# Near scores of a pair in one step, far turns in pairs, and group weights through main memory

## The chip, the cores and the metric

One core of one Trainium2 chip. The metric is the device time of the whole kernel in microseconds, the median of the runs; beside it stands one profiled execution, with its own time and its span (first to last instruction). TensorE's clock was granted nearly in full throughout (0.99 to 1.00 in every stretch read here, the level of 2.4 GHz).

## The reference, cut to what matters

A decoder trunk of two residual layers on 512 tokens of 1024 features. Layer 0 mixes tokens by pooling, layer 1 by attention; each is followed by a SwiGLU feed-forward block. Only the attention of layer 1 matters here.

```python
ATTN_PATTERNS = ((128, 1), (512, 4), (2048, 16))       # window, dilation; heads 0-5, 6-10, 11-15
def attn_mixer(h, w_qkv, w_out):
    ...
    q = rope(qkv[:, :, 0]) * HEAD_DIM ** -0.5
    k = rope(qkv[:, :, 1])
    v = qkv[:, :, 2]
    for (window, dilation), n_g in zip(ATTN_PATTERNS, HEAD_GROUPS):
        o_g, lse_g = dilated_window_attention(q[:, :, sl], k[:, :, sl], v[:, :, sl], window, dilation)
        outs.append(o_g)
        lses.append(jax.nn.logsumexp(lse_g, axis=-1) - math.log(n_g))
    alpha = jax.nn.softmax(jnp.stack(lses, axis=-1), axis=-1)
    merged = jnp.concatenate([o_g * (N_ATTN_GROUPS * alpha[:, :, g])[:, :, None, None] for g, o_g in enumerate(outs)], axis=2)
    ...
    return jnp.einsum('bse,ed->bsd', merged, w_out)
```

So every token has a softmax within each head (window of 128 for the near heads 0 to 5; every fourth token for the far heads 6 to 10, every sixteenth for 11 to 15), and a weight for each of the three groups of heads (alpha), which multiplies that group's outputs.

## The kernel before

All large products run as three fp32r products of parts (high x high, low x high, high x low), so TensorE has about three times the plain work; a weight tile is loaded by SP (L104), its high part cast by ScalarE (L137), its low part taken by VectorE (L138). TensorE's order is the order of the program text (L76). The order on VectorE, ScalarE and POOL is the planner's, which starts from the program's order and a model of when things are ready.

Attention is laid out in **steps**, one per projection. Steps 0 to 15 project q and k of the eight head pairs t (step 2t for q, 2t+1 for k, L962 to L973): `project` (L226) is 24 matmuls of 512 columns into one of four PSUM banks of the pool `mm`. `rope` (L812) takes such a bank: VectorE shuffles and multiplies, POOL multiplies (L817), VectorE adds. Steps 16 to 18 project v for the near heads, steps 19 to 26 the far heads' v in two parts of four steps with 320 columns. After each step `later` (L929) puts some of the attention's own work on TensorE between the projections:

- **Scores.** `near_scores` (L840) runs for pairs t = 0, 1, 2 in two halves, blocks 0 and 1 at step 2t+3 and blocks 2 and 3 at step 2t+4, each half with two banks of the pool `psc` (which has two). VectorE adds the mask (L859, L865) and takes the row maxima (L862, L863, L869). `far_scores` (L873) does a far pair (t = 3 to 7) at step 2t+3 with the same two banks.
- **Softmax.** `soften` (L832): VectorE negates the maxima (L835), ScalarE takes exponentials (L837). One step later `normalise` (L896): VectorE takes reciprocals, POOL multiplies (L902 for near heads, L904 for far ones).
- **Turns.** `transposes` (L907), one step after that at the earliest: seven blocks of a near head or four of a far head are turned by TensorE through the pool `ptr` (two banks, four blocks each) and copied to `pT` by ScalarE for even heads (L925), by VectorE for odd ones (L923). `later` takes one head per step, in the order of the heads: steps 6 to 21.
- **Values.** `turn` (L1045) turns the near heads' v tiles at steps 17, 18 and 19 through `ptr` as well, ahead of `later`; ScalarE copies them (L1050).
- **Group weights.** At step 20 `group_sums` (L979), at step 22 `group_weights` (L999): VectorE computes `gw`, 12 columns for each token, and POOL copies each group's four columns out to 512 (L1019). At step 24 `spread_weights` (L1023) multiplies these by the identity on TensorE (L1028), and ScalarE copies the results to `LB`, which then holds each token's weight on all partitions (L1031).

Then (L1090 on) each pair's outputs are products of v and pT, which VectorE multiplies by `LB` (L1112 near, L1115 far); they are split (L312, L313) and go into the output projection (L352 to L354), and the feed-forward block follows.

Of the kernel before, what the change touches and what calls it, by code (L numbers as in the profile page):

```python
# [10 lines left out]
F32 = mybir.dt.float32  # L11
# [6 lines left out]
P = 128  # L18
S = 512
# [38 lines left out]
def trunk_kernel(ctx: ExitStack, tc: tile.TileContext, x_in, xT, gam, gains, consts, ident_d, w0, wT, w1, wv, w_down, out):  # L58
# [731 lines left out]
    with ExitStack() as actx:  # L790
        ap = actx.enter_context(tc.tile_pool(name="attn", bufs=1, reuse_waits="tile"))
        work = ExitStack()
        aw = work.enter_context(tc.tile_pool(name="attnw", bufs=2, reuse_waits="tile"))
        psc = actx.enter_context(tc.tile_pool(name="psc", bufs=2, space=bass.MemoryType.PSUM))
# [45 lines left out]
        def near_scores(t, half, q, k):  # L840

            pair = (2 * t, 2 * t + 1)
            if half == 0:
                state[t] = [aw.tile([P, 4, 256], F32, name="e", bufs=4) for _ in pair]
            scs = [psc.tile([P, 4, P], F32, name="sc").rearrange("p b k -> p (b k)") for _ in pair]
            for b in (2 * half, 2 * half + 1):
                at = (b % 2) * 256
                lo = max(b - 1, 0) * P
                for i, scf in enumerate(scs):
# [6 lines left out]
            for h, scf, e in zip(pair, scs, state[t]):  # L856
                flat = e.rearrange("p b k -> p (b k)")
                if half == 0:
                    nc.vector.scalar_tensor_tensor(  # L859
                        flat[:, P : 4 * P], scf[:, P : 4 * P], HD ** -0.5, masks[:, 0 : 3 * P], op0=ALU.mult, op1=ALU.add  # L860
                    )
                    nc.vector.tensor_reduce(mx[:, h, 0:1], e[:, 0, P:], axis=AX.X, op=ALU.max)  # L862
                    nc.vector.tensor_reduce(mx[:, h, 1:2], e[:, 1, :], axis=AX.X, op=ALU.max)  # L863
                else:
                    nc.vector.scalar_tensor_tensor(  # L865
                        e[:, 2:4, :], scf.rearrange("p (b k) -> p b k", b=2), HD ** -0.5,
                        masks[:, P : 3 * P].unsqueeze(1).to_broadcast([P, 2, 2 * P]), op0=ALU.mult, op1=ALU.add,
                    )
                    nc.vector.tensor_reduce(mx[:, h, 2:4], e[:, 2:4, :], axis=AX.X, op=ALU.max)  # L869
                    got.append((h, *soften(h, e, [e[:, b, (P if b == 0 else 0) : 256] for b in range(4)])))  # L870
# [58 lines left out]
        def later(step):  # L929

            if pend_tr and pend_tr[0][0] <= step:
                transposes(*pend_tr.pop(0)[1:])
# [29 lines left out]
        for t in range(8):  # L962
# [7 lines left out]
            if t < 3:  # L970
                pend_sc += [(at, near_scores, (t, 0, q, k)), (at + 1, near_scores, (t, 1, q, k))]
            else:
                pend_sc.append((at, far_scores, (t, q, k)))  # L973
# [3 lines left out]
        state["perm"] = ap.tile([P, 4, 2], F32, name="gperm")  # L977

# [20 lines left out]
        def group_weights():  # L999
# [8 lines left out]
            w = ap.tile([P, 3, 4], F32, name="gw")  # L1008
# [7 lines left out]
            bcs = []  # L1016
            for g in range(3):
                bc = aw.tile([P, S], F32, name="ropeb" if g == 2 else "ropea").rearrange("p (b j) -> p b j", b=4)
                nc.gpsimd.tensor_copy(bc, w[:, g, :].unsqueeze(2).to_broadcast([P, 4, P]))  # L1019
                bcs.append(bc)  # L1020
            return bcs

        def spread_weights(bcs):  # L1023

            for g, bc in enumerate(bcs):
                tp = psc.tile([P, 4, P], F32, name="sc") if g == 2 else ptr.tile([P, 4, P], F32, name="tp")
                for b in range(4):
                    nc.tensor.matmul(tp[:, b, :], lhsT=bc[:, b, :], rhs=ident, start=True, stop=True)  # L1028

                to = LB[g].rearrange("p (j r) -> p r j", r=R) if g == 0 else LB[g].rearrange("p (r j) -> p r j", r=R)  # L1030
                nc.scalar.copy(to, tp)  # L1031
# [159 lines left out]
```

## Time and profile before

| what | value |
|---|---|
| median of 3 runs | 1018.32 us (1017.35 to 1019.07) |
| the profiled execution | 1018.4 us, span 1016.6 us |
| TensorE busy | 1000.0 us (98%) |
| VectorE busy | 792.8 us (78%) |
| ScalarE busy | 530.0 us (52%) |
| POOL busy | 121.0 us (12%) |
| HBM read | 151.99 MB |
| the chain that ended last | 92% TensorE, 3% VectorE, 2% DMA, 2% ScalarE |

The span starts with layer 0 (to about 455 us), then come the attention (to about 680 us, its output projection among it) and the feed-forward block of layer 1. The shares are means over stages with different limits; the attention's steps, from 481 to 621 us, are where the changed lines stand. Times in a timeline are counted from the span's start. A matmul's duration in a row includes its way through the array, so the pitch from one start to the next says what it costs, not the duration.

### The profile page before, as it was taken

How to read it: one execution, taken by the hardware profiler on the slowest of the kernel's cores; microseconds unless marked ns; L12 is line 12 of the kernel's file. 1: busy time of each engine (PE TensorE's matmuls, PEld its weight loads, DVE VectorE, ACT ScalarE, POOL GpSimd, SP SyncE). 2: the span in 40 equal slices, each digit the busy share in tenths (PEclk: the TensorE clock that was granted, in tenths of full speed). 3: DMA queues.
4: the chain of work that ended last, by engine and by line, in shares of the span. 5: the costliest groups of instructions: out<-in, count | busy, mean ns of one | idle time of the engine just before them, and what ended most of it. 6: DMA issues, size and time to landing. Idle time of an engine off the chain costs nothing.

```text
span 1016.6 us, 16615 instructions
## 1 busy us (share of the span) xinstructions
PE 1000.0 (98%) x6582; PEld 912.5 (90%) x6582; DVE 792.8 (78%) x1134; ACT 530.0 (52%) x836; POOL 121.0 (12%) x108
## 2 busy tenths in 40 slices
PE   9999989999999999999999999999999999999997
PEld 7888879989998998989777899889998999999895
DVE  6483689898888788777988747569989888888875
ACT  5572467545654554463344444357654564455454
POOL 0000101101011100001333210100101001111000
PEclk9999989999999999999999999999999999999999
DMA  9451467759559854514311246525866955975522
GB/s 346 157 186 21 117 194 193 175 170 260 142 129 248 222 142 139 183 57 145 103 42 52 75 124 175 116 63 160 203 150 192 237 149 118 287 187 138 154 71 83
DMA packets 76349, 155.16 MB, mean 153 GB/s; under 512 B 6448, under 2 KB 6576, under 8 KB 76272
## 3 DMA queue, kind: packets, MB, share of 16 engines
q1 hardware_dynamic: 58944, 121.00, 35.5%
q0 software_dynamic: 17040, 32.84, 19.1%
q8 instruction: 51, 0.84, 0.3%
q10 hardware_dynamic: 288, 0.27, 0.1%
q14 instruction: 26, 0.21, 0.1%
HBM read 151.99 MB, written 2.10 MB: 152 GB/s over the span
## 4 chain that ended last, share of the span: by engine, by line
PE 92%; DVE 3%; DMA 2%; ACT 2%; issue 1%; POOL 0%; SPq 0%; ACTq 0%; POOLq 0%
PE p L601 24%; PE r L601 13%; PE r L684 10%; PE mm L601 6%; PE p L684 5%; PE mm L222 4%; PE mm L224 3%; PE mm L223 3%; PE mm L738 3%; PE mm L684 2%; PE mm L354 2%; PE mm L352 2%; PE mm L353 2%; DMA vraw<-w 1%; PE mm L1073 1%; PE mm L1072 1%
## 5 line engine op out<-in xcount | busy, mean ns | idle before, releaser
L138 DVE TENSOR_TENSOR wlo<-wraw,whi 128x1024 fp32r<-128x1024 f32 (+2 forms) x190 | 220.4, 1161 | 76.6 <-ACT whi L137 76.0
L137 ACT CAST whi<-wraw 128x1024 fp32r<-128x1024 f32 (+2 forms) x190 | 185.2, 978 | 173.0 <-issue 34.7
L137 ACT CAST whi<-vraw 128x1024 fp32r<-128x1024 f32 (+1 forms) x102 | 99.4, 976 | 148.0 <-DVE vraw L140 51.6
L601 PE MATMUL p<-t_hi,wlo 128*128 128x256 f32 x528 | 149.9, 284 | 0.0
L601 PE MATMUL p<-t_lo,whi 128*128 128x256 f32 x528 | 149.9, 284 | 0.0
L601 PE MATMUL p<-t_hi,whi 128*128 128x256 f32 x528 | 148.7, 282 | 0.9 <-ACT ct L616 0.9
L138 DVE TENSOR_TENSOR wlo<-vraw,whi 128x1024 fp32r<-128x1024 f32 (+1 forms) x102 | 114.9, 1127 | 19.8 <-ACT whi L137 19.3
L601 PE MATMUL r<-h_hi,whi 128*128 128x256 f32 x352 | 100.3, 285 | 3.9 <-ACT h_hi L312 3.9
L601 PE MATMUL r<-h_lo,whi 128*128 128x256 f32 x352 | 101.1, 287 | 0.1
L601 PEld LDWEIGHTS p<-t_hi,whi 128*128 128x128 f32 x528 | 100.1, 189 | 1.1 <-ACT ct L616 1.1
L601 PE MATMUL r<-h_hi,wlo 128*128 128x256 f32 x352 | 101.0, 287 | 0.0
L601 PEld LDWEIGHTS p<-t_hi,wlo 128*128 128x128 f32 x528 | 99.8, 189 | 0.0
L601 PEld LDWEIGHTS p<-t_lo,whi 128*128 128x128 f32 x528 | 99.3, 188 | 0.1
L106 POOL DMA_DIRECT2D wraw<-w x22 | 26.8, 1216 | 429.3 <-DMA wraw<-w 93.2
L140 DVE TENSOR_TENSOR vraw<-vraw,wraw 128x1024 f32<-128x1024 f32 x68 | 76.6, 1127 | 0.8
L601 PEld LDWEIGHTS r<-h_hi,whi 128*128 128x128 f32 x352 | 67.9, 193 | 4.1 <-ACT h_hi L312 4.1
L601 PEld LDWEIGHTS r<-h_lo,whi 128*128 128x128 f32 x352 | 67.4, 191 | 0.4 <-DVE h_lo L313 0.4
L601 PEld LDWEIGHTS r<-h_hi,wlo 128*128 128x128 f32 x352 | 67.6, 192 | 0.0
L222 PE MATMUL mm<-h_hi,whi 128*128 128x512 f32 (+1 forms) x176 | 65.3, 371 | 0.0
L224 PE MATMUL mm<-h_hi,wlo 128*128 128x512 f32 (+1 forms) x176 | 63.6, 361 | 0.0
L223 PE MATMUL mm<-h_lo,whi 128*128 128x512 f32 (+1 forms) x176 | 63.5, 361 | 0.0
L684 PE MATMUL r<-wlo,u_hi 128*128 128x512 f32 x144 | 56.1, 390 | 0.0
(313 smaller groups left out, 2516.4 us busy)
## 6 DMA issues: line engine op xcount, KB each, us to landing
wraw<-w SPq DMA_DIRECT2D x116, 512.0 KB, 4.9
wraw<-w_down SPq DMA_DIRECT2D x32, 512.0 KB, 3.7
wraw<-w POOLq DMA_DIRECT2D x22, 512.0 KB, 7.5
vraw<-w SPq DMA_DIRECT2D x22, 512.0 KB, 5.0
vraw<-w POOLq DMA_DIRECT2D x22, 512.0 KB, 8.9
wraw<-wT SPq DMA_DIRECT2D x16, 512.0 KB, 3.8
wraw<-w_down SPq DMA_DIRECT2D x24, 256.0 KB, 2.7
vraw<-w_down SPq DMA_DIRECT2D x6, 512.0 KB, 5.4
```

The costliest lines, as they stand in the source:

```text
L106: nc.gpsimd.dma_start(dst, more, accum_op=ALU.add)
L137: nc.scalar.copy(hi[:, :n], raw[:, :n])
L138: nc.vector.tensor_sub(lo[:, :n], raw[:, :n], hi[:, :n].bitcast(F32))
L140: nc.vector.tensor_add(raws[into][:, :n], raws[into][:, :n], raws[more][:, :n])
L222: nc.tensor.matmul(ps, lhsT=whi, rhs=xhi, start=first, stop=False, **kw)
L223: nc.tensor.matmul(ps, lhsT=whi, rhs=xlo, start=False, stop=False, **kw)
L224: nc.tensor.matmul(ps, lhsT=wlo, rhs=xhi, start=False, stop=last, **kw)
L352: nc.tensor.matmul(ps, lhsT=xhi, rhs=w[0][:, k, :], start=first, stop=False)
L353: nc.tensor.matmul(ps, lhsT=xhi, rhs=w[1][:, k, :], start=False, stop=False)
L601: nc.tensor.matmul(ps[:, g, :], lhsT=w[:, g, c, :], rhs=xx[:, c, :], start=i in (0, 1, 3) and g + c + k == 0, stop=c == 3 and k == 2, skip ...
L684: nc.tensor.matmul(acc[t], lhsT=u, rhs=w, start=i in (0, 1, 3) and c + k == 0, stop=c == len(pairs) - 1 and k == 2, skip_group_check=True,)
L738: nc.tensor.matmul(ps, lhsT=u, rhs=w[:, m, :], start=z + m + k == 0, stop=z == 1 and m == 1 and k == 2,)
```

## The change

Three things change in the attention, and nothing outside it.

1. A near pair is scored in one step (2t+3) with four banks: two of `psc` and two of `mm`. Masks and maxima follow per head; one reduction covers blocks 1 to 3. A near head's turn can therefore come one step earlier (steps 5 to 10).
2. `later` turns up to two heads per step where they are far heads: pairs t = 3 to 7 at steps 11, 13, 15, 17 and 19, which is two steps behind their scores.
3. The group weights are computed at step 21. At step 22 one transpose brings them to 12 rows of 128 (group and residue x token), ScalarE copies these, a DMA on POOL's queue stores them in main memory, and three more on that queue load each group's 512 values onto all 128 partitions. The values now stand by residue for all three groups, so the near heads' multiply reads and writes with a stride.

```diff
--- before.py
+++ after.py
@@ -791,6 +791,7 @@
         ap = actx.enter_context(tc.tile_pool(name="attn", bufs=1, reuse_waits="tile"))
         work = ExitStack()
         aw = work.enter_context(tc.tile_pool(name="attnw", bufs=2, reuse_waits="tile"))
+        dram = actx.enter_context(tc.tile_pool(name="dram", bufs=1, space=bass.MemoryType.DRAM))
         psc = actx.enter_context(tc.tile_pool(name="psc", bufs=2, space=bass.MemoryType.PSUM))
         ptr = actx.enter_context(tc.tile_pool(name="ptr", bufs=2, space=bass.MemoryType.PSUM))
 
@@ -837,37 +838,37 @@
                 nc.scalar.activation(blk, blk, AF.Exp, bias=neg[:, b : b + 1], accum_out=den[:, h, b : b + 1])
             return e, blocks
 
-        def near_scores(t, half, q, k):
+        def near_scores(t, q, k):
 
             pair = (2 * t, 2 * t + 1)
-            if half == 0:
-                state[t] = [aw.tile([P, 4, 256], F32, name="e", bufs=4) for _ in pair]
-            scs = [psc.tile([P, 4, P], F32, name="sc").rearrange("p b k -> p (b k)") for _ in pair]
-            for b in (2 * half, 2 * half + 1):
+            banks = [
+                [(psc.tile([P, 4, P], F32, name="sc") if half == 0 else mm.tile([P, S], F32, name="mm").rearrange("p (b k) -> p b k", b=4)) for _ in pair]
+                for half in range(2)
+            ]
+            banks = [[sc.rearrange("p b k -> p (b k)") for sc in scs] for scs in banks]
+            for b in range(4):
                 at = (b % 2) * 256
                 lo = max(b - 1, 0) * P
-                for i, scf in enumerate(scs):
+                for i, scf in enumerate(banks[b // 2]):
                     rows = slice(HD * i, HD * i + HD)
                     nc.tensor.matmul(
                         scf[:, at + (P if b == 0 else 0) : at + 256], lhsT=q[rows, b * P : (b + 1) * P],
                         rhs=k[rows, lo : (b + 1) * P], start=True, stop=True,
                     )
             got = []
-            for h, scf, e in zip(pair, scs, state[t]):
+            for i, h in enumerate(pair):
+                e = aw.tile([P, 4, 256], F32, name="e", bufs=4)
                 flat = e.rearrange("p b k -> p (b k)")
-                if half == 0:
-                    nc.vector.scalar_tensor_tensor(
-                        flat[:, P : 4 * P], scf[:, P : 4 * P], HD ** -0.5, masks[:, 0 : 3 * P], op0=ALU.mult, op1=ALU.add
-                    )
-                    nc.vector.tensor_reduce(mx[:, h, 0:1], e[:, 0, P:], axis=AX.X, op=ALU.max)
-                    nc.vector.tensor_reduce(mx[:, h, 1:2], e[:, 1, :], axis=AX.X, op=ALU.max)
-                else:
-                    nc.vector.scalar_tensor_tensor(
-                        e[:, 2:4, :], scf.rearrange("p (b k) -> p b k", b=2), HD ** -0.5,
-                        masks[:, P : 3 * P].unsqueeze(1).to_broadcast([P, 2, 2 * P]), op0=ALU.mult, op1=ALU.add,
-                    )
-                    nc.vector.tensor_reduce(mx[:, h, 2:4], e[:, 2:4, :], axis=AX.X, op=ALU.max)
-                    got.append((h, *soften(h, e, [e[:, b, (P if b == 0 else 0) : 256] for b in range(4)])))
+                nc.vector.scalar_tensor_tensor(
+                    flat[:, P : 4 * P], banks[0][i][:, P : 4 * P], HD ** -0.5, masks[:, 0 : 3 * P], op0=ALU.mult, op1=ALU.add
+                )
+                nc.vector.scalar_tensor_tensor(
+                    e[:, 2:4, :], banks[1][i].rearrange("p (b k) -> p b k", b=2), HD ** -0.5,
+                    masks[:, P : 3 * P].unsqueeze(1).to_broadcast([P, 2, 2 * P]), op0=ALU.mult, op1=ALU.add,
+                )
+                nc.vector.tensor_reduce(mx[:, h, 0:1], e[:, 0, P:], axis=AX.X, op=ALU.max)
+                nc.vector.tensor_reduce(mx[:, h, 1:4], e[:, 1:4, :], axis=AX.X, op=ALU.max)
+                got.append((h, *soften(h, e, [e[:, b, (P if b == 0 else 0) : 256] for b in range(4)])))
             return got
 
         def far_scores(t, q, k):
@@ -928,8 +929,12 @@
 
         def later(step):
 
-            if pend_tr and pend_tr[0][0] <= step:
-                transposes(*pend_tr.pop(0)[1:])
+            for _ in range(2):
+                if pend_tr and pend_tr[0][0] <= step:
+                    h, e = pend_tr.pop(0)[1:]
+                    transposes(h, e)
+                    if HEAD_GROUP[h] == 0:
+                        break
             while pend_nm and pend_nm[0][0] <= step:
                 _, h, e, blocks = pend_nm.pop(0)
                 pend_tr.append((step + 1, h, normalise(h, e, blocks)))
@@ -967,14 +972,12 @@
             k = rope(pk, t, "k")
             later(2 * t + 1)
             at = 2 * t + 3
-            if t < 3:
-                pend_sc += [(at, near_scores, (t, 0, q, k)), (at + 1, near_scores, (t, 1, q, k))]
-            else:
-                pend_sc.append((at, far_scores, (t, q, k)))
+            pend_sc.append((at, near_scores if t < 3 else far_scores, (t, q, k)))
 
         LB = [ap.tile([P, S], F32, name=f"LB{g}") for g in range(3)]
         state["sums"] = ap.tile([P, 2, 3, 4], F32, name="gsums")
         state["perm"] = ap.tile([P, 4, 2], F32, name="gperm")
+        state["w"] = ap.tile([P, 3, 4], F32, name="gw")
 
         def group_sums():
 
@@ -1005,7 +1008,7 @@
             nc.vector.tensor_max(top, top, ms[:, 0, 2, :])
             nc.vector.tensor_sub(ms[:, 0, :, :], ms[:, 0, :, :], top.unsqueeze(1).to_broadcast([P, 3, 4]))
             nc.scalar.activation(ms[:, 0, :, :], ms[:, 0, :, :], AF.Exp)
-            w = ap.tile([P, 3, 4], F32, name="gw")
+            w = state["w"]
             for g, n in enumerate(GROUP_HEADS):
                 nc.vector.scalar_tensor_tensor(w[:, g, :], ms[:, 1, g, :], 1.0 / n, ms[:, 0, g, :], op0=ALU.mult, op1=ALU.mult)
             nc.vector.tensor_add(top, w[:, 0, :], w[:, 1, :])
@@ -1013,31 +1016,26 @@
             nc.vector.reciprocal(top, top)
             for g in range(3):
                 nc.vector.scalar_tensor_tensor(w[:, g, :], w[:, g, :], float(len(GROUP_HEADS)), top, op0=ALU.mult, op1=ALU.mult)
-            bcs = []
+
+        def spread_weights():
+
+            tp = ptr.tile([P, 4, P], F32, name="tp")
+            nc.tensor.transpose(tp[:12, 0, :], state["w"].rearrange("p g r -> p (g r)"), ident)
+            rows = aw.tile([P, S], F32, name="ropea")[:, :P]
+            nc.scalar.copy(rows[:12, :], tp[:12, 0, :])
+            far = dram.tile([12, P], F32, name="far")
+            nc.gpsimd.dma_start(far, rows[:12, :])
             for g in range(3):
-                bc = aw.tile([P, S], F32, name="ropeb" if g == 2 else "ropea").rearrange("p (b j) -> p b j", b=4)
-                nc.gpsimd.tensor_copy(bc, w[:, g, :].unsqueeze(2).to_broadcast([P, 4, P]))
-                bcs.append(bc)
-            return bcs
-
-        def spread_weights(bcs):
-
-            for g, bc in enumerate(bcs):
-                tp = psc.tile([P, 4, P], F32, name="sc") if g == 2 else ptr.tile([P, 4, P], F32, name="tp")
-                for b in range(4):
-                    nc.tensor.matmul(tp[:, b, :], lhsT=bc[:, b, :], rhs=ident, start=True, stop=True)
-
-                to = LB[g].rearrange("p (j r) -> p r j", r=R) if g == 0 else LB[g].rearrange("p (r j) -> p r j", r=R)
-                nc.scalar.copy(to, tp)
+                nc.gpsimd.dma_start(LB[g], far[4 * g : 4 * g + 4, :].rearrange("(o r) j -> o (r j)", o=1).partition_broadcast(P))
 
         def between(step):
             later(step)
             if step == 20:
                 group_sums()
+            if step == 21:
+                group_weights()
             if step == 22:
-                state["bcs"] = group_weights()
-            if step == 24:
-                spread_weights(state["bcs"])
+                spread_weights()
 
 
         to_turn = []
@@ -1108,11 +1106,9 @@
                     continue
                 rows = slice(0, P) if both else slice(HD * (h % 2), HD * (h % 2) + HD)
                 al = LB[HEAD_GROUP[h]]
-                if h < 6:
-                    nc.vector.tensor_mul(o[rows, :], ps[rows, :], al[rows, :])
-                else:
-                    by_r = lambda z: z[rows, :].rearrange("p (r j) -> p r j", r=R)
-                    nc.vector.tensor_mul(o[rows, :].rearrange("p (j r) -> p r j", r=R), by_r(ps), by_r(al))
+                by_r = lambda z: z[rows, :].rearrange("p (r j) -> p r j", r=R)
+                in_turn = lambda z: z[rows, :].rearrange("p (j r) -> p r j", r=R)
+                nc.vector.tensor_mul(in_turn(o), in_turn(ps) if h < 6 else by_r(ps), by_r(al))
             split(m_hi[:, t, :], m_lo[:, t, :], o)
         norm = Norm(2, mp.tile([P, D], F32, name="even_rows"))
         sc_tile = lambda: psc.tile([P, 4, P], F32, name="sc")
```

## Rows read from the trace of the kernel before

**Rows 1.** Windows: length; busy us (and instructions) of each engine; clock, DMA share, GB/s
```profile
480.00:541.93 61.93, 60.34 (x322) 47.24 (x320) 55.19 (x104) 27.35 (x80) 21.85 (x17) 1.00 0.21 70
640.00:1016.60 376.60, 369.48 (x2518) 343.98 (x2516) 303.30 (x411) 200.50 (x278) 36.55 (x32) 0.99 0.58 152
```
**Rows 2.** Timeline of TensorE (start, us, engine, line, operation): steps 4 and 7
```profile
482.53 0.50 PE L222 MATMUL mm<-h_hi,whi 128*128 128x512 f32 x1
489.27 0.50 PE L222 MATMUL mm<-h_hi,whi 128*128 128x512 f32 x1
...
504.09 0.39 PE L222 MATMUL mm<-h_hi,whi 128*128 128x512 f32 x1
...
508.64 0.39 PE L224 MATMUL mm<-h_hi,wlo 128*128 128x512 f32 x1
```
**Rows 3.** Timeline of TensorE: the spread at step 24 and the next product
```profile
611.06 1.95 PE L1028 MATMUL tp<-ident,ropea 128*128 128x128 f32 x16
...
613.65 0.39 PE L1072 MATMUL mm<-whi,h_hi 128*128 128x320 f32 x1
```
**Rows 4.** Timeline of TensorE: its two waits, at steps 8 and 11
```profile
517.02 0.70 PE L851 MATMUL sc<-k,q 64*128 64x256 f32 x2
518.36 1.13 PE L851 MATMUL sc<-k,q 64*128 64x256 f32 x6 [0.65 <-DVE e L859]
...
539.93 0.98 PE L920 MATMUL tp<-ident,e 128*128 128x128 f32 x7 [0.94 <-ACT pT L925]
```
**Rows 5.** VectorE by line (ns min/median/max; the split's row: total, mean ns)
```profile
L859 DVE SCALAR_TENSOR_TENSOR e<-sc,gain x6: 527/546/599, 483.9 to 517.8; 128x384 f32<-128x384 f32 x6
L862 DVE TENSOR_REDUCE mx<-e x6: 253/276/285, 485.6 to 519.4; 128x1 f32<-128x128 f32 x6
L863 DVE TENSOR_REDUCE mx<-e x6: 403/406/411, 485.8 to 519.6; 128x1 f32<-128x256 f32 x6
L869 DVE TENSOR_REDUCE mx<-e x6: 667/669/678, 493.6 to 525.5; 128x2 f32<-128x512 f32 x6
L138 DVE TENSOR_TENSOR wlo<-wraw,whi 128x1024 fp32r<-128x1024 f32 (+2 forms) x190 | 220.4, 1161 | 76.6 <-ACT whi L137 76.0
```
**Rows 6.** Timelines of TensorE and ScalarE: value turns at steps 17 and 19
```profile
579.70 0.60 PE L1049 MATMUL tp<-ident,ropea 128*128 128x128 f32 x4
580.82 0.59 ACT L1050 COPY v<-tp 128x512 f32<-128x512 f32 x1
591.72 0.60 PE L1049 MATMUL tp<-ident,ropea 128*128 128x128 f32 x4
592.55 0.58 ACT L1050 COPY v<-tp 128x512 f32<-128x512 f32 x1
```
**Rows 7.** Landing of a store (L759) and a POOL load (L961); weights; multiplies
```profile
DMA to landing us min/median/max: 2.0/2.0/2.0
DMA to landing us min/median/max: 4.0/4.0/4.0
598.98 1.17 POOL L1019 COPY ropea<-gw 128x512 f32<-128x512 f32 x2 [9.82 <-DVE gw L1015]
623.79 0.69 DVE L1112 TENSOR_TENSOR o<-mm,LB 128x512 f32<-128x512 f32 x1 [0.52 <-PE mm L1103]
L1115 DVE TENSOR_TENSOR o<-mm,LB x6: 1056/1078/1122, 629.4 to 638.0; 128x512 f32<-128x512 f32 x4, 64x512 f32<-64x512 f32 x2
```
**Rows 8.** Timelines: POOL's products, and TensorE's first product behind far scores
```profile
498.17 2.97 POOL L902 TENSOR_TENSOR e<-e,rden 128x768 f32<-128x768 f32 x2 [0.96 <-DVE rden L899]
526.96 0.50 PE L222 MATMUL mm<-h_hi,whi 128*128 128x512 f32 x1
539.95 1.05 POOL L904 TENSOR_TENSOR e<-e,rden 128x512 f32<-128x512 f32 x1
555.05 0.50 PE L222 MATMUL mm<-h_hi,whi 128*128 128x512 f32 x1
565.15 1.05 POOL L904 TENSOR_TENSOR e<-e,rden 128x512 f32<-128x512 f32 x1
```

## The prediction

> **What bounds the kernel now.** I read the busy time of the engines over the attention stretch first, then TensorE's own order of work, and only then the engines that feed it. TensorE works almost without a break: in [rows 1] it is busy for 60.34 of the 61.93 us in which the near pairs are scored, and 369.48 of 376.60 us behind the attention. So a microsecond of TensorE's work or waiting taken out of the attention should reach the end nearly whole. The reader is to see a second thing in the same row: VectorE is busy 55.19 of those 61.93 us. It is the engine that could take over there, and TensorE's waits in this stretch [rows 4] are waits for what VectorE delivers late. Before the near pairs and after the last far pair nothing of the kind shows.
>
> **The change part by part.** All sums are against the profiled execution: 1018.4 us, of which 1016.6 us are the span. The median of the runs is 1018.32 us, 0.08 us lower, so a sum carries over as it is.
>
> *Spreading the group weights.* TensorE loses 24 matmul pieces, from 611.06 to 613.65 [rows 3]: 2.59 us, 0.108 us a piece. It gains one transpose, one such piece, with its own way in and out of the fp32 work (some 0.03 us in all by the same rows, as 24 pieces leave no room for more). I take 2.59 - 0.11 - 0.03 = **2.45 us** gained. The three copies on POOL and the three on ScalarE that go lie beside TensorE's work; I cost them at nothing.
>
> *The broadcast.* Instead the weights go ScalarE copy, store to main memory, three loads, the four DMAs one behind the other on POOL's queue. No row shows that pair of transfers; the nearest ones are a store that landed in 2.0 us and a 320 KB load from POOL's queue that landed in 4.0 us [rows 7] (the new loads are 256 KB each). The group weights are ready at 598.98 [rows 7], where POOL begins to copy them. Even if the transpose came no earlier than the old spread at 611.06, the copy (0.59 us, like the one in [rows 6]), the store and the first load would end at 611.06 + 0.11 + 0.59 + 2.0 + 4.0 = 617.8, and its place is two part-projects earlier. The first reader is VectorE's multiply at 623.79 [rows 7]. At least 6 us of cover, so nothing on the path. If the cover were gone, VectorE's multiplies would wait, then the PSUM banks they free, then TensorE. What is queued behind these DMAs on POOL is the accumulating weight loads of the FFN, which start later. TensorE's multiplications don't see the new strided multiply for heads 0 to 5 either: it goes from 0.69 us to at most about the 1.08 us of the far heads' form [rows 7], 3 x 0.39 = 1.2 us on VectorE, beside products that read finished tiles. One rule speaks against this part. Rows 7 show one POOL load alone, nothing about what VectorE does to it. The Trainium skill, "SBUF — State Buffer", section "SBUF: two separate sides", says that a DMA issued from POOL's queue can be kept from writing its descriptors while VectorE runs certain copies, and advises another queue. No row here shows that; by an estimate of one 0.69 us instruction ahead of each of the four DMAs it would make the rows some 2.8 us later, and leave the sum as it is.
>
> *Near scores in one step.* Each pair is scored at step 2t+3 alone instead of in halves at two steps. The products are the same. What goes is one entry and exit per pair: 24 products of a projection have a pitch of (508.64 - 504.09)/20 = 0.2275 us, 5.46 us in all [rows 2]. The step with a second half lasts from 482.53 to 489.27, 6.74 us, so the half costs 1.28 us, while its 8 pieces at 0.107 are 0.86. The difference, 0.42 us, is the separate block's own price; three pairs give **1.26 us**. Bounds: 0.2 us a pair, if the second half's long exit stays with the merged block, to 0.42.
>
> *VectorE's part of it.* One reduction over 256 columns (0.406 us) and one over 512 (0.669 us) [rows 5] become one over 768. Their difference, 0.263 us for 256 columns, makes that 0.93 us: 0.14 us less a head, 0.85 us over six heads, none of it on the path by itself.
>
> *Waits that should go.* Two stalls of TensorE stand in the rows [rows 4]. At 517.02 two pieces are issued, then none until 518.36, where the row names VectorE's first mask: 1.34 - 2 x 0.107 = 1.13 us. The cause is that a half takes both score banks again one step after the half before it. With four banks a pair comes back to the same two banks only two steps later, so this goes. At 539.93 a transpose waits 0.94 us for ScalarE's copy of the head before; that copy stands behind the exponentials of the first far pair, which VectorE let start late. Near work ends one step earlier after the change, and the last near head turns at step 10, before those exponentials. I take both: **2.07 us**. Bounds: 1.13 to 2.07.
>
> *Banks.* The two further banks come from the four that projections use. A projection then waits for the rope of two projections ago instead of four. VectorE's backlog would have to exceed 5.5 us before that costs anything, and the rows of masks and reductions [rows 5] come to some 2 to 2.5 us a head. I cost it at nothing; without that cover it would be the excess of the backlog, a microsecond at most.
>
> *Far turns in pairs.* Both heads of a far pair turn at one step, every second step. The transposes are the same; that fewer entries are made I cost at nothing (0 to 0.15 us). But at steps 17 and 19 the turn of a value tile comes first, and three tiles then want two banks. The third waits for ScalarE's copy of the first. At step 17 the turn starts at 579.70 and the copy runs 580.82 + 0.59 = 581.41 [rows 6]; the third tile would be wanted at 579.70 + 8 x 0.108 = 580.57, so **0.85 us** are lost. At step 19 the turn starts at 591.72, the copy ends at 592.55 + 0.58 = 593.13, the third tile is wanted at 592.58: **0.55 us**. In sum 1.4 us lost; between 0 (if ScalarE takes the copy first) and 2.5.
>
> *The deadline.* Turns now come exactly two projections behind the scores: about 11.0 us, plus 0.43 us for the second head, whose first head turns ahead of it. Near pairs: today the chain from the second half's scores (over at 489.27) to POOL's first finished head (498.17 + 2.97/2 = 499.66) is 10.4 us [rows 2, 8]. In it the masks stand in program order behind the next projection's rope and a weight split (1.16 us a split [rows 5]); now they stand ahead of both, and that makes up for the first half's 0.546 + 0.276 + 0.406 = 1.23 us of that head, so I expect 10 to 11 us. In the steady far stretch the scores end at 555.05 and POOL's last product at 565.15 + 1.05 = 566.20 [rows 8]: 11.15 us against 11.4, just in time. I put **0.5 us** down for misses; bounds 0 and the rival below.
>
> Sum: 2.45 + 1.26 + 2.07 - 1.4 - 0.5 = 3.9 us gained, 1018.4 - 3.9 = **1014.5 us**.
>
> **The rivals.** *The masks queue as they do now.* The near chain of 10.4 us has the first half's masks outside it. If VectorE handles all masks of the pair before the first maximum, 2 x 1.23 = 2.46 us come on top: 12.85 us against 11.0, a miss of 1.85 us. Three pairs: up to 5.5 us, though the later two have another head's seven transposes (0.75 us) in the time available. The first far pair, with scores ending at 526.96 and POOL at 539.95 + 1.05 = 541.00, takes 14.0 us today [rows 8] against about 12.2. That would be 4 to 5 us of new stalls and eat the gain: **1018.6 us**. For it: VectorE is 89% busy there, its order is a planner's, and today it lets a weight split pass between a pair's masks. Against: the masks' place in program order and the work taken away.
>
> *VectorE becomes the bound, and it is slower.* The same place, but each of six pairs' masks (three near, three far) has another weight split (1.16 us [rows 5]) ahead of it in VectorE's queue, which today falls into the slack between halves. Then the misses are 5 + 6 x 1.16 = 12 us: 1018.4 + 12 + 1.4 - 5.8 = 1026 us at full price, where 5.8 us is the sum of the gains and 1.4 us the value tiles' loss, and about **1022 us** if two thirds of it happen. It decides from the point at which the misses exceed 4.4 us (5.8 - 1.4); past 6.4 us it shows as slower. For it speaks that VectorE has only 6.7 us of slack in 61.93; against, that the same work fits today with two stalls of 2.07 us.
>
> *The change does only what the trace proves.* Stalls neither go nor come: 1018.4 - 2.45 - 1.26 = **1014.7 us**, close enough to the forecast to share its range. *No new stall at all*: 1018.4 - 5.8 = **1012.6 us**. *The broadcast is late* by over 6 us: each microsecond beyond costs one, **1020 us**.
>
> **How the numbers follow.** Forecast, with the rival that shares its range: 0.58 (1013 to 1016.2). No new stall: 0.09. Masks queue as now: 0.20, mostly within 0.2% (2 us, about what a measurement of this kernel can tell from no change). VectorE bound: 0.10. Broadcast late: 0.03. Faster: 0.58 + 0.09 = 0.67; same 0.21, most of the queueing case; slower 0.12. The range reaches from 1012.0 (no new stall, with the 0.15 us of fewer entries and up to 0.4 us in the 0.85 us that VectorE saves) to 1018.8, the whole of the queueing case; left out are the slower cases and a little below.
>
> **What would show it.** The spread's pieces gone and one transpose in their place (right by construction, 2.4 us). Three blocks of 16 score pieces of about 1.9 us, with no wait between. No idle at the fourth near scores or at the fourth head's copy. A wait of 0.5 to 0.9 us for the value tile's copy at each of steps 17 and 19. The three broadcasts landed before the first multiply. Wrong: waits of transposes for POOL at steps 5 to 15 that sum to over 3 us (the queueing case), projections that wait for rope (banks), or multiplies that wait for a DMA.

## The result, and the profile after

The changed kernel takes 1022.24 us (median of 6 runs, 1020.37 to 1023.65), the kernel before 1018.16 us beside it: a ratio of **1.0036, interval 1.0023 to 1.005**. It is slower by some 3.7 us, where 3.9 us less were forecast. The gains came as forecast (5.8 us, seen in the run g3 below); what failed is a term that stood in the sum with 0.5 us.

A stretch of TensorE's timeline places it better than the whole time does: from the first score product of step 3 to the first output product. Each kernel has one profiled execution, so a length has no interval of its own; but the stretch begins anywhere from 480.39 to 483.56 us in the fourteen profiles, though no edit touches what lies ahead of it, while waits that several kernels share come out alike (the one at step 5 below: 0.72 to 0.75 us in eight kernels). In the kernel before this is 620.86 - 481.68 = 139.18 us. In the changed kernel (timeline of TensorE: start, us, engine, line, operation):

```profile
482.74 0.49 PE L854 MATMUL sc<-k,q 64*128 64x128 f32 x4
...
625.15 0.32 PE L1099 MATMUL mm<-pT,v 128*64 128x128 f32 x1
```

That is 142.41 us, 3.23 us more. The profiled spans differ by 3.9 us: a further 1.06 us lie ahead of the stretch (482.74 against 481.68), in the first matmuls of the kernel, which the change doesn't touch (see the end), and 0.4 us less lie behind it. The lengths below are all of this stretch.

Where the 3.23 us come from is seen in what TensorE waited for, first as its weight loads' waits in the stretch (us in total, times, longest):

```profile
PEld tp L921 <- DVE pT L924: 2.8, 3, 1.0
PEld tp L921 <- POOL e L905: 2.7, 1, 2.7
PEld tp L921 <- issue: 1.8, 2, 1.0
PEld tp L921 <- DVE e L902: 1.1, 1, 1.1
```

Every large one ends at a transpose (L921): TensorE is ready to turn a head, and the head or the bank is not. Then one by one, with the releaser in brackets; these answer [rows 4] and [rows 6]:

```profile
496.38 0.98 PE L921 MATMUL tp<-ident,e 128*128 128x128 f32 x7 [0.73 <-DVE e L902]
...
511.34 0.66 PE L921 MATMUL tp<-ident,e 128*128 128x128 f32 x4 [0.34 <-DVE pT L924]
512.80 0.55 PE L921 MATMUL tp<-ident,e 128*128 128x128 f32 x3 [0.81 <-DVE pT L924]
...
528.24 0.55 PE L921 MATMUL tp<-ident,e 128*128 128x128 f32 x3 [0.80 <-DVE pT L924]
...
544.77 0.66 PE L921 MATMUL tp<-ident,e 128*128 128x128 f32 x4 [2.51 <-POOL e L905]
...
587.11 0.63 PE L921 MATMUL tp<-ident,e 128*128 128x128 f32 x4 [0.82 <-ACT v L1048]
...
599.85 0.63 PE L921 MATMUL tp<-ident,e 128*128 128x128 f32 x4 [0.52 <-ACT v L1048]
```

Steps 5, 7, 9, 11, 17 and 19. The two waits of [rows 4] are gone, and waits at six steps stand in their place. The last two are the value tiles' copies, as forecast. The windows around step 11 show a second cost (length; busy us and instructions of PE, PEld, DVE, ACT, POOL; granted clock, DMA share, GB/s):

```profile
541.66:545.36 3.70, 1.19 (x9) 0.78 (x7) 3.38 (x7) 1.53 (x2) 2.51 (x2) 1.00 0.17 16
545.36:549.00 3.64, 3.64 (x22) 3.03 (x22) 3.12 (x6) 0.00 (x0) 0.58 (x1) 0.55 0.21 78
```

A far pair's eight transposes take 3.70 us up to the scores behind them, against 0.96 us at step 13 of the same kernel (559.06 to 560.02): 2.7 us of waiting. Behind them the granted clock is at about half, the lower of its two levels (1.2 GHz), for 3.6 us: the scores take 1.72 us instead of 1.09 and the two next projections 11.98 us instead of 11.02, 1.6 us together. Step 11 costs 4.3 us in all.

The parts that were to gain did gain. The spread is one transpose (0.27 us in its row, 0.02 us to the next product's start), and the broadcast was in time: its store landed 3.5 us after issue, its loads 6.5 to 7.5 us after theirs, the last at 617.6 + 7.5 = 625.1 at the latest, before the first multiply at 629.48. These answer [rows 7] and [rows 3]:

```profile
L1023 PE MATMUL tp<-ident,gw x1: 271/271/271, 610.9 to 610.9; 128*12 128x128 f32 x1
...
DMA to landing us min/median/max: 3.5/3.5/3.5
...
L1029 POOL DMA_DIRECT2D LB<-far x3: 544/544/577, 616.5 to 617.6; - x3
...
DMA to landing us min/median/max: 6.5/7.0/7.5
...
629.48 2.06 DVE L1111 TENSOR_TENSOR o<-mm,LB 128x512 f32<-128x512 f32 x2
```

VectorE's rows answer [rows 5]: the merged reduction takes 0.938 us (0.93 forecast).

```profile
L870 DVE TENSOR_REDUCE mx<-e x6: 935/938/944, 488.5 to 522.5; 128x3 f32<-128x768 f32 x6
```

### The profile page after: what moved, and what is told of

Read it like the earlier page. It is cut to its first block, busy times and chain, and to the rows that moved or that the text cites. A ratio compares the mean times of both kernels' runs of the same rounds, so it can differ in the third digit from the quotient of the medians.

```text
span 1020.5 us, 16564 instructions
## 1 busy us (share of the span) xinstructions
PE 999.7 (98%) x6559; PEld 911.9 (89%) x6559; DVE 796.1 (78%) x1128; ACT 529.0 (52%) x834; POOL 125.1 (12%) x109
## 4 chain that ended last, share of the span: by engine, by line
PE 89%; DVE 5%; ACT 2%; DMA 2%; issue 2%; POOL 1%; SPq 0%; POOLq 0%; DVEq 0%; ACTq 0%
PE p L601 24%; PE r L601 13%; PE r L684 10%; PE mm L601 6%; PE p L684 5%; PE mm L222 3%; PE mm L738 3%; PE mm L223 3%; PE mm L224 3%; PE mm L684 2%; PE mm L352 2%; PE mm L354 2%; PE mm L353 2%; DMA vraw<-w 1%; PE early L223 1%
## 5 line engine op out<-in xcount | busy, mean ns | idle before, releaser
L684 PE MATMUL r<-whi,u_lo 128*128 128x512 f32 x144 | 56.1, 390 | 0.0
```

Of the source, the lines that this page charges most:

```text
L684: nc.tensor.matmul(acc[t], lhsT=u, rhs=w, start=i in (0, 1, 3) and c + k == 0, stop=c == len(pairs) - 1 and k == 2, skip_group_check=True,)
```

## The experiments

**The two theories.** A: the merged near step costs the time, since the masks of a whole pair stand in VectorE's queue at once and what TensorE needs stands behind them. B: the turns of far heads in pairs cost it, since two projections are too short a deadline for both heads. The planner orders VectorE, ScalarE and POOL anew for every kernel, so an edit can also move instructions that it doesn't name; at two places below (g2 and g3) that is seen to matter. The lengths, and the time against the kernel before in the same set of runs (the two agree to 1.4 us in every row):

| kernel | parts | stretch, us | time ratio (interval) |
|---|---|---|---|
| before | | 139.18 | 1 |
| changed | all three | 142.41 | 1.0036 (1.0023 to 1.005) |
| e1 | near step | 139.04 | 1.0002 (0.9988 to 1.0016) |
| e2 | far pairs | 142.28 | 1.0035 (1.0022 to 1.0049) |
| e3 | spread | 136.60 | 0.9974 (0.9961 to 0.9987) |
| e4 | near step, spread | 136.49 | 0.9987 (0.9975 to 1.0) |
| f1 | e4, near copies on ScalarE | 135.36 | 0.9964 (0.9949 to 0.9979) |
| f2 | changed, far turns a step later | 136.98 | 0.998 (0.9965 to 0.9995) |
| f3 | changed, value tiles in other banks | 139.12 | 1.0012 (0.9995 to 1.0029) |
| f4 | changed, with all three of these | 135.28 | 0.9961 (0.9946 to 0.9975) |
| g1 | changed, all turns a step later, value banks | 135.62 | 0.996 (0.9946 to 0.9975) |
| g2 | changed, near copies on ScalarE | 137.79 | 0.9987 (0.9976 to 0.9999) |
| g3 | f1, near divisions on ScalarE too | 133.37 | 0.9948 (0.9934 to 0.9961) |
| h1 | changed, both on ScalarE, value banks | 134.39 | 0.9948 (0.9935 to 0.9962) |

**The parts alone: e1 to e4.** Each takes the kernel before and makes the named parts of the change, as they stand in the diff.

> The kernel before with the near scores in one step over four banks, and nothing else of the change: far heads turn one per step, the weights are spread by TensorE. Theory A (the merged near step is what costs: it lets the masks of a whole pair stand in VectorE's queue at once, and the odd near heads' copies to pT late): the stalls seen with the whole change at steps 5 to 9 come back, 0.9 + 0.5 + 1.15 + 1.05 = 3.6 us, against 1.26 us of score blocks and 1.13 us of the old wait gone: about 1.2 us slower than before, 1019.4. Theory B (the turns of far heads in pairs are what costs: the first pair is not ready at step 11, TensorE waits 2.8 us and its granted clock falls afterwards): without the pairs the near part gains its 1.26 us and up to 2.07 us of waits, 1015 to 1017.

e1: 139.04 us, no change in time. Both theories are half right: the price of the score blocks and both old waits do go, and the new waits eat that. They are the same as in the changed kernel, so they come from the near step alone (its timeline of TensorE at step 7):

```profile
508.99 0.65 PE L920 MATMUL tp<-ident,e 128*128 128x128 f32 x4 [0.34 <-DVE pT L923]
510.45 0.55 PE L920 MATMUL tp<-ident,e 128*128 128x128 f32 x3 [0.81 <-DVE pT L923]
```

> The kernel before with the far heads' turns in pairs, and nothing else of the change. Theory B: the first far pair is scored at step 9 with VectorE later than in the changed kernel (near work there ends one step later), so the wait at step 11 is at least as long: about 3 us of wait, 1.5 us at the lower clock, and 1.6 us at steps 17 and 19 for the value tile's copy, less the 0.94 us wait that was there: some 5 us slower, 1023. Theory A: the pairs cost only the 1.6 us at steps 17 and 19 and what was missed by a few tenths: 1019.5 to 1020.

e2: 142.28 us, 3.1 us more, and 0.35% in time. The wait is at step 13, not at step 11: here the last near head still turns at step 11, and the first far pair follows it at step 12. The second pair is late:

```profile
553.95 0.60 PE L920 MATMUL tp<-ident,e 128*128 128x128 f32 x4
555.79 0.66 PE L920 MATMUL tp<-ident,e 128*128 128x128 f32 x4 [1.24 <-POOL e L904]
```

With the block at 2.43 us instead of 0.97 (its own step 15), that is 1.5 us, and steps 17 and 19 cost 1.0 and 0.7 us. So B holds for the far pairs, with another pair than expected and without the lower clock.

> The kernel before with the group weights spread through main memory (computed at step 21, transposed at step 22), and nothing else of the change. Both theories: 24 pieces of 0.108 us less one, 2.45 us faster, 1015.7. If the broadcast were late after all, the multiplies would wait for its DMAs and the gain would shrink or turn: 1017 or more. In the changed kernel the last load landed some 4 us before the first multiply.

e3: 136.60 us, 2.58 us less (2.45 expected), and a time ratio of 0.9974. The spread is a gain by itself.

> The changed kernel with one far head turned per step as before. Theory A: the near stalls of 3.6 us stay, the 2.45 us of the spread are gained: about 1017. Theory B: everything the change was to gain without the pairs, 2.45 + 1.26 us and up to 2.07 us of waits: 1012.5 to 1014.5.

e4: 136.49 us, e1 and e3 together. The three parts alone add up to -0.14 + 3.10 - 2.58 = +0.4 us; together they cost 3.23. The rest, 2.8 us, is step 11, which costs 4.3 us where e2 loses 1.5 at step 13. There near and far work meet: with the near step merged, the first far pair is to turn one step earlier than in e2, in the stretch in which VectorE is still late.

**What exactly is late: f1 to f4.** Three edits, to `transposes` (f1, f4, and later g2, g3 and h1), to `later` (f2, f4) and to `turn` (f3, f4, and later g1 and h1), in this order:

```diff
-                if h % 2:
+                if h % 2 and h >= 6:
                     nc.vector.tensor_copy(pT[:, at : at + n, :], tp[:, :n, :])
...
-                pend_tr.append((step + 1, h, normalise(h, e, blocks)))
+                pend_tr.append((step + 1 + (h >= 6), h, normalise(h, e, blocks)))
...
-            tp = ptr.tile([P, 4, P], F32, name="tp")
+            tp = mm.tile([P, S], F32, name="mm").rearrange("p (b j) -> p b j", b=4) if m < 2 else psc.tile([P, 4, P], F32, name="sc")
```

> The merged near step and the spread through main memory, far heads one per step (the run e4), with ScalarE instead of VectorE copying the odd near heads' turned blocks. Lengths are from the first scores of step 3 to the first output product: 139.18 us before, 142.41 in the changed kernel, 136.49 in e4. Theory: at steps 7 and 9 TensorE waits for PSUM banks, since VectorE's copies of the odd head before stand behind the masks of a whole pair. Then the 1.65 us at step 7 and the 1.05 us at step 9 go: 133.8 us, and 2.7 us less time than e4. Rival: the banks were only the first of the late things, the head's own softmax is as late, and its wait takes their place: 135.5 us or more.

f1: 135.36 us, 1.1 us less than e4. The wait at step 7 goes, as the theory has it. The one at step 9 comes back from the other engine; ScalarE's copies now stand behind its own exponentials and a weight cast (the rival's shape, at a bank; timelines of TensorE and ScalarE):

```profile
524.54 0.98 PE L921 MATMUL tp<-ident,e 128*128 128x128 f32 x7 [1.12 <-ACT pT L926]
...
522.97 1.03 ACT L137 CAST whi<-wraw 128x1024 fp32r<-128x1024 f32 x1
523.91 0.95 ACT L926 COPY pT<-tp 128x512 f32<-128x512 f32 x2
```

> The changed kernel with the far pairs' turns one step later (three steps behind their scores, at steps 12, 14, 16, 18 and 20), still in pairs. Theory: the deadline of two projections is what the first pair misses; a step more is enough. The wait of 2.8 us at step 11 goes, with it 0.6 us of scores and 0.9 us of products at the lower clock, and one of the two waits for a value tile's copy (step 18 has one, step 20 none): 142.41 - 4.3 - 0.8 = 137.3 us. Rival: VectorE is too far behind for either, the wait moves to steps 12 to 14: over 140 us.

f2: 136.98 us (137.3 expected). A step more is enough for the far pairs: no wait for POOL is left, each pair's block takes 0.79 us (a projection follows it here, not scores), one wait for a value tile remains at step 18.

> The changed kernel with the turned value tiles in banks of other pools (projections' banks at steps 17 and 18, a score bank at step 19), so that a far pair finds both turn banks free. Theory: the waits of steps 17 and 19, 1.05 and 0.65 us, are for the bank that ScalarE's copy of the value tile frees: 142.41 - 1.7 = 140.7 us. Rival: the odd head's product on POOL is late there too: 142 us.

f3: 139.12 us, 3.3 us less, where 1.7 were expected. Steps 17 and 19 lose their waits, as expected. The other 1.6 us are the clock: the wait at step 11 is the same, 2.53 us, but here the granted clock stays up behind it. That may be luck of the one profiled execution: the ten runs of f3 reach from 1015.34 to 1024.20 us, and the ratio of 1.0012 is some 1.2 us more than before, as a length of 140.4 us would be.

```profile
541.59:545.31 3.72, 1.19 (x9) 0.78 (x8) 3.40 (x7) 1.53 (x2) 2.51 (x2) 1.00 0.13 14
545.31:549.00 3.69, 3.69 (x28) 3.14 (x28) 3.58 (x6) 0.00 (x0) 0.58 (x1) 1.00 0.21 79
```

> The changed kernel with all three: near copies on ScalarE, far pairs one step later, value tiles in other banks. If the three waits are independent, 142.41 - 2.7 - 4.3 - 1.7 = 133.7 us, 5.5 us less than before, some 1012 us. If VectorE's load is the one cause and the waits only move, 137 us or more.

f4: 135.28 us. The waits are not independent; the near ones move, the far ones and the value tiles' go. The change's order of steps now beats the kernel before, with about 2 us of near waits left.

**Deadline or queue: g1 to g3 and h1.** In g1 the edit to `later` reads `step + 2` for every head.

> The changed kernel with every head's turn one step later, near and far (near heads at steps 6 to 11, far pairs at steps 12 to 20), and the value tiles' turns in other banks; copies as in the changed kernel. Theory: it is the deadline of two projections that fails, for near and far alike, and a pair's work fits if a turn may come three steps behind. Then no wait is left: the length from the first scores of step 3 to the first output product falls to 133 us (139.18 before, 142.41 changed), 6 us less time than before. Rival: the near waits are for banks that VectorE's late copies hold; the copies are as late relative to the next turn, and 1 to 2.7 us stay: 134 to 136 us.

g1: 135.62 us, the rival's. A later turn removes the wait at step 5, where a head itself was late, and leaves the waits for banks, which now read ScalarE's copies. So more time alone doesn't mend the near steps; clearing VectorE's queue does (g3).

> The changed kernel with ScalarE copying the odd near heads' turned blocks, everything else as changed (far pairs at step 11 on). Theory: the first far pair is late since its reciprocal stands in VectorE's queue behind a rope and two such copies (1.23 us), so besides the near waits (1.65 us at step 7) the wait at step 11 shrinks by 1 us or more, from 2.5 us to 1.5 us or less. Rival: POOL or the exponentials set that time, and the wait at step 11 stays at 2.5 us.

g2: 137.79 us. With the six copies of three near heads off VectorE's queue, the first far pair's wait at step 11 falls from 2.51 to 0.33 us, without touching the far pair itself, and the clock stays up:

```profile
539.39 0.60 PE L921 MATMUL tp<-ident,e 128*128 128x128 f32 x4
540.32 0.66 PE L921 MATMUL tp<-ident,e 128*128 128x128 f32 x4 [0.33 <-POOL e L905]
```

> The run f1 (merged near step, spread through main memory, far heads one per step, near copies on ScalarE), with the division of a near head's first block done by ScalarE instead of VectorE, where it runs for up to 1.6 us while POOL divides the other blocks. Theory: at step 5 TensorE waits for that instruction, which stands in VectorE's queue behind a rope's addition that runs 2.3 us beside POOL; then the 0.9 us at step 5 go and the wait of 1.3 us at step 9 shrinks: 133.5 to 134.5 us (f1 135.36). Rival: POOL's own division of the other blocks is as late, and the length stays at 135 us or more.

g3 takes f1 and replaces one line in `normalise`:

```diff
-            nc.vector.tensor_scalar_mul(blocks[0], blocks[0], rden[:, 0:1])
+            nc.scalar.activation(blocks[0], blocks[0], AF.Copy, scale=rden[:, 0:1])
```

133.37 us, and a ratio of 0.9948: the best of all, 5.3 us faster than the kernel before. All waits over half a microsecond are gone, the one at step 9 too, though ScalarE has more work than in f1. At step 9 the planner's order has part in that: the weight cast that stood ahead of the copies in f1 now stands behind them (525.82).

```profile
524.39 0.39 ACT L902 ACTIVATE e<-e,rden 128x128 f32<-128x128 f32 x1
524.68 0.94 ACT L926 COPY pT<-tp 128x512 f32<-128x512 f32 x2
```

> The changed kernel whole (far pairs two steps behind their scores, too), with ScalarE copying the odd near heads' turned blocks and dividing a near head's first block, and the value tiles' turns in other banks. Theory: what failed was the order of small instructions in VectorE's queue, not the deadline as such; with 12 copies and 6 divisions off that queue every wait goes, the one of the first far pair at step 11 too: 133.0 to 133.5 us from the first scores of step 3 to the first output product (142.41 changed, 137.79 with the copies alone), and no more than 0.2 us better than with far heads one per step (133.37). Rival: the far pair's deadline is too short in itself, and 0.7 us at step 11 and some tenths at step 13 stay: 134 us or more.

h1: 134.39 us, the rival's by length. What moved are six copies and six divisions (the expectation counts twelve copies). The whole change with them runs at 0.9948 as well, so near step and spread pay once VectorE's queue is cleared. But at step 11 a wait of 0.74 us for POOL is left, and some 0.3 us at step 13:

```profile
537.24 0.60 PE L921 MATMUL tp<-ident,e 128*128 128x128 f32 x4
538.59 0.66 PE L921 MATMUL tp<-ident,e 128*128 128x128 f32 x4 [0.74 <-POOL e L905]
```

So for the first far pair the deadline is short in this order too. Its scores end at 525.41, but VectorE's masks start at 530.60, with two weight splits ahead of them (525.69 and 528.05), and POOL's second product starts at 537.50, behind a rope's. Whether another order would make it fit was not tried. Turning far heads in pairs buys nothing here: g3, which leaves it out, is as fast in time and 1.0 us shorter in the stretch.

## Why the prediction was wrong

**What bounds the kernel.** Right: TensorE's order sets the end, and microseconds gained or lost in the stretch reach the end. VectorE was named as the engine that could take over. The new waits do come from its queue; that it lacks time for the work itself is not shown, for g3 takes only twelve small instructions from it.

**Spread, score blocks, old waits.** Right in size. Forecast were 2.45 + 1.26 + 2.07 = 5.78 us of gains; g3, in which they stand with only tenths of new waits, is 139.18 - 133.37 = 5.81 us shorter. e3 gives the spread alone 2.58 us, which leaves 3.23 us for the other two (3.33 forecast); these two were not taken apart. The broadcast was covered, with some 4 us to spare instead of 6: its transfers took 3.5 and 6.5 to 7.5 us to land, where the nearest rows gave 2.0 and 4.0. The rule of the Trainium skill ("SBUF — State Buffer", section "SBUF: two separate sides"), that VectorE's copies can keep POOL's descriptors from being written, would have been seen as a delay. The three loads were issued in 0.54 to 0.58 us each, no longer than the one POOL load of before (L961, 0.61 us), so the trace shows none at issue; what made the landings long no run here separates.

**Value tiles.** Right: 1.4 us forecast; 1.0 us at step 17 (the block takes 1.97 us instead of 0.97) and 0.7 us at step 19, and f3 removes both.

**The deadline: the step that failed.** It stood in the sum with 0.5 us, reasoned from when a head's *data* would be ready. Measured were 3.2 us at the near steps (the changed kernel from step 3's scores to the first far scores is 528.72 - 482.74 = 45.98 us, g3 42.83) and 4.3 us at step 11: 2.7 of wait, and 1.6 at the lower clock, for which the sum had no term. With the 1.7 us of the value tiles that is 9.2 us lost against 5.8 gained, 3.4 us net, where the stretch measured 3.23. Three things were missing from the deadline.

First, the forecast's chain ended with POOL's product and left out the division of a head's first block, which is VectorE's. The first pair's masks do run ahead of the weight split, as forecast (484.97 to 490.55, the split from 490.47), but that division has its own place in VectorE's queue. In the changed kernel step 5's transpose waits for L902, which stands behind a rope's addition that itself runs 2.33 us beside POOL's division (timelines of VectorE and POOL):

```profile
492.90 0.17 DVE L900 RECIPROCAL rden<-den 128x4 f32<-128x4 f32 x1
493.89 2.33 DVE L827 TENSOR_TENSOR q<-ropea,ropeb 128x512 f32<-128x512 f32 x1 [0.82 <-POOL ropeb L818]
496.06 0.26 DVE L902 TENSOR_SCALAR e<-e,rden 128x128 f32<-128x128 f32 x1
...
493.81 1.47 POOL L903 TENSOR_TENSOR e<-e,rden 128x768 f32<-128x768 f32 x1
```

The head's exponentials were done in time (its reciprocal ran at 492.90), and POOL's own part at 495.28. Only the 0.26 us on VectorE came 3.2 us behind the reciprocal, when TensorE had been ready for some 0.6 us. g3 moves it to ScalarE, and the wait goes.

Second, the *banks of the turn* were not in the sum at all. The odd head's copies are VectorE's; head 1 is turned from 504.59 on, and its two banks are read here:

```profile
506.32 0.94 DVE L870 TENSOR_REDUCE mx<-e 128x3 f32<-128x768 f32 x1
...
507.65 0.18 DVE L900 RECIPROCAL rden<-den 128x4 f32<-128x4 f32 x1 [0.19 <-ACT e L838]
507.86 1.59 DVE L902 TENSOR_SCALAR e<-e,rden 128x128 f32<-128x128 f32 x1
...
510.61 0.68 DVE L924 COPY pT<-tp 128x512 f32<-128x512 f32 x1
...
512.20 0.55 DVE L924 COPY pT<-tp 128x384 f32<-128x384 f32 x1
```

The next head is to turn at 510.84, by TensorE's order, and needs both. In the kernel before the same copies run between the masks of two halves, and the second ends half a microsecond ahead of the next turn:

```profile
515.06 0.55 DVE L923 COPY pT<-tp 128x384 f32<-128x384 f32 x1
516.16 0.92 PE L920 MATMUL tp<-ident,e 128*128 128x128 f32 x7
```

The forecast had looked at the projections' banks, which indeed never mattered, and at the two banks of the turn only where three tiles meet.

Third, at step 11 the far pair's second reciprocal (L900) is served 2.2 us after its exponentials end (at 540.32), behind a rope and the copies of a near head (timelines of ScalarE and VectorE):

```profile
540.13 0.19 ACT L838 ACTIVATION_READ_ACCUMULATOR e<-e,neg 128x1 f32 x1
...
538.81 0.18 DVE L900 RECIPROCAL rden<-den 128x4 f32<-128x4 f32 x1 [1.65 <-ACT e L838]
...
540.14 0.68 DVE L924 COPY pT<-tp 128x512 f32<-128x512 f32 x1
541.47 0.69 DVE L822 TENSOR_TENSOR q<-ropea,ropeb 128x512 f32<-128x512 f32 x1 [0.65 <-POOL ropeb L818]
542.07 0.55 DVE L924 COPY pT<-tp 128x384 f32<-128x384 f32 x1
542.54 0.17 DVE L900 RECIPROCAL rden<-den 128x4 f32<-128x4 f32 x1
```

g2 takes the copies out, and 2.2 us of the wait go, where the two copies are 1.2 us of work. The rest is order: with the copies gone, the planner puts the reciprocal ahead of the rope's addition, before which VectorE sits idle until POOL's product is there. It is served 1.55 us behind the first one (536.65) instead of 3.73:

```profile
538.20 0.18 DVE L900 RECIPROCAL rden<-den 128x4 f32<-128x4 f32 x1
539.30 1.51 DVE L822 TENSOR_TENSOR q<-ropea,ropeb 128x512 f32<-128x512 f32 x1 [0.93 <-POOL ropeb L818]
```

Before all that the pair's masks were late: its scores ended at 529.81, and the masks ran from 534.49, again behind two weight splits (528.19 and 531.94).

**The rivals.** The first, masks that queue, foresaw the place and most of the size (4 to 5 us of stalls; 5.9 us came), but gave 1018.6 us, since it left the clock and the banks out. The sign named for it was waits for POOL over 3 us; they sum to 2.51 us, and those for VectorE's division and copies to 2.7. The second, slower one (1022 us) came nearest in time, in part by luck: its two thirds of 12 us are all weight splits and masks, while 1.6 us of what came are the clock, and the waits at steps 5, 7 and 9 go when a division and copies move. Its picture is in the trace too: two weight splits stand ahead of the second pair's masks, whose scores were over at 499.01.

```profile
497.95 1.21 DVE L138 TENSOR_TENSOR wlo<-wraw,whi 128x1024 fp32r<-128x1024 f32 x1
...
500.32 2.03 DVE L138 TENSOR_TENSOR wlo<-wraw,whi 128x1024 fp32r<-128x1024 f32 x1
...
502.87 0.55 DVE L862 SCALAR_TENSOR_TENSOR e<-sc,gain 128x384 f32<-128x384 f32 x1
```

No run took a split away, so what they cost by themselves stays open. What came is the case that the two rivals had at 0.30 together. The row that spoke for it was in the forecast: VectorE 89% busy where it would be asked for a pair's masks at once. The 5.8 us of gain were read from single rows, the 0.5 us from a chain across four engines with 0.3 us to spare, and the second was given no more doubt than the first.

## What to carry to other kernels

Where an engine is near 90% busy, an instruction's cost to those who wait is its place in that engine's queue, not its duration: twelve small instructions of six heads, moved to an engine that was over half idle (ScalarE, 27.35 of 61.93 us busy in [rows 1]), were worth 3.1 us here (e4 to g3, with what the planner made of it), more than any of the three parts of the change gained. A schedule that asks for a result sooner should be checked for every small thing on the way, the copies that free a buffer included, and parts that are to be tried are best tried alone: one of the three gained, one was even, and one lost.

## What the runs showed of the hardware

A wait of the same length behind the same work may or may not cost the clock. Behind 2.51 us of waiting at step 11 of the changed kernel TensorE's granted clock was 0.55 over the next 3.6 us, 1.6 us lost; behind 2.53 us in f3 it was 1.00. What decides between the two was not tried.

At its start the changed kernel's profile shows products of layer 0 at a pitch of 0.43 us up to 9.63 us, the one of before 0.23 us for the same products; by then it is 1.7 us behind, and 1.06 us of that are left at the stretch. The pitch is that of the products at a granted clock of 0.50 at step 11 (547.08 to 549.00), but here the profile gives the granted clock as 1.00, so what slowed them stays open.

VectorE and POOL ran long beside each other here: the division of a 128 x 128 block on VectorE takes 0.26 us alone (496.06) and 1.59 us where POOL divides the other blocks (507.86); a weight split takes 1.21 us alone (497.95) and 2.03 us beside a rope's product on POOL (500.32, POOL from 499.97), which is another tile; and POOL's division took up to 2.36 us (512.91) instead of 1.47.
